# Copies of the attention's key pages, made at other places of a decoder step

## The chip, the cores and the metric

The kernel runs on one core of a Trainium2 chip. The core has five engines that work side by side, each in its own order: TensorE (PE in the profile) multiplies matrices, VectorE (DVE) and ScalarE (ACT) work element by element, GpSimd (POOL) does this more slowly and issues some DMAs, and SyncE (SP) issues most DMAs. The metric is the time of one execution in microseconds, lower is better; a kernel's time is the median of its runs.

## The reference

One inference step of a decoder layer, for a prompt of 1024 tokens and for 8 running sequences with 4 new tokens each (32 "sample" rows, 1056 rows in all). Model width is 1024, everything is in float32. What matters here:

```python
h, gate = modulated_input(x, c, w_ada, b_ada, g_norm)
qa, ka, va, za, qi, ki, wi, qr, kr, vr, zr, ga, gr = split_projection(h @ w_in)
y_a = attn_fn(heads(qa), ka, va, heads(qi), ki, wi) * silu(za)     # sparse attention, 8 heads of 64
ret, ret_state = ret_fn(rotary(qr), rotary(kr) * DK_R ** -0.5, vr) # retention, 8 heads of 64
y_r = group_norm_heads(ret) * g_ret * silu(zr)
merged = sigmoid(ga) * (y_a @ w_pa) + sigmoid(gr) * (y_r @ w_pr)
x = x + gate * (merged @ w_out)
```

The sparse attention scores all keys with a small indexer (4 heads of 64), keeps the best 256 of each query and attends to these. For the sample rows the past keys and values lie in a pool of 80 pages of 128 tokens; a page table of 8 sequences times 8 pages says which page holds what:

```python
ki_past = cache_kidx[page_table].reshape(DB, PAST_LEN, HEAD_DIM_IDX)
kg = where(in_past, cache_k[phys, slot], take_rows(k_new, idx_n))   # phys from page_table
logits = einsum('bqhd,bqkhd->bhqk', q, kg) * HEAD_DIM_A ** -0.5
```

## The kernel before, in words

Each projection is one block of 128 of the weight columns, made for all 1056 rows in three chunks of 352. A product in float32 is made of three products of rounded parts (high times high, low times high, high times low; L226 to L228), so a projection takes 72 matrix products. Its weights are loaded one projection ahead by SyncE (`prefetch`, L205) into two or three buffers and split into their high and low part by ScalarE (L211) and by VectorE or, for every third, GpSimd (L212). `project_parts` runs the chunks and hands each to a function `use(c, p)` that empties the bank.

The stages follow each other in this order, with the times of the profiled execution. The head (0 to 54 us) normalizes and modulates the rows and makes the first projections. The index stage (66 to 140 us) scores the prompt's keys block by block, from row block 7 down to 2, with four heads each (L905 to L915); beside it four gate projections run, and GpSimd gathers the samples' index keys page by page (L951). Retention (145 to about 545 us) runs over four pairs of heads; each has the projections of the attention's queries, of the retention's keys, queries, values and gate, and of two merge gates, 7 projections or 21 chunks, between which its own products stand: score products (L739), products with the state, and at the end of the pair the group norm (L802 to L824), whose rows are turned by TensorE (L821) and multiplied out of the bank by VectorE (L824). Rotation (L691 to L693) is done by GpSimd for the first two pairs and for the keys of the third. In the same stage VectorE and ScalarE count, bit by bit, the threshold of the best 256 scores (`pick_all`; L996 on VectorE, L1003 on ScalarE), one bit behind every two chunks. Then come four key projections and four value projections (560 to 690 us). Between them the samples' past keys are scored: SyncE reads the gathered keys back (L1210), VectorE turns them in blocks of 32 (L1212), TensorE multiplies (L1195), in eight groups of four sequences times a quarter of the past. Gates, the prompt's attention, and the output follow.

The past keys are not read from the pool directly. `copy_page` copies one page of a sequence, 256 KB, from the pool into a scratch array KG in device memory, in the order of blocks in which the keys are read back later. It takes three steps: ScalarE writes one column of the page table into a small tile with two buffers (L582), GpSimd loads the number of the sequence from it into a register (L583), and GpSimd issues the DMA from the page of that number (L584). `project_parts` calls it behind every chunk from the start of retention on, so the 64 copies run behind the first 64 chunks of retention's 84, sequence by sequence. What was left of them would be made ahead of the samples' key stage, by a loop that finds nothing to do.

The order of each engine's instructions is laid out when the kernel is built: a planner takes the instructions in the order of the program text as priorities and places each on its engine as its model of durations lets it be ready. `tc.issue_after(x)` forbids an instruction to be placed ahead of `x` on the same engine; in `copy_page` it keeps ScalarE's write behind the last ScalarE instruction that the program made so far. `marks` keeps the search's steps behind the chunks in the same way.

Of the kernel before, what the change touches and what calls it, by code (L numbers as in the profile page):

```python
# [124 lines left out]
def _hybrid_step(ctx, tc, A, outs, dbg):  # L125
    nc = tc.nc
# [17 lines left out]
    def pj():  # L144

        turns[0] += 1
        if third[0] and turns[0] % 3 == 0:
            return third[0].tile([128, 512], F32, name="pj3", bufs=1)
        return psj.tile([128, 512], F32, name="pj", bufs=2)

    def pl():
        return ps.tile([128, 1024], F32, name="pl", bufs=2)

    def pt():
        return ps.tile([128, 512], F32, name="pt", bufs=2)
# [68 lines left out]
    def terms(p, w, k, sl):  # L224
        wh, wl = w
        nc.tensor.matmul(p, wh[:, k], HH[k][:, sl], start=(k == 0), stop=False)  # L226
        nc.tensor.matmul(p, wh[:, k], HL[k][:, sl], start=False, stop=False)  # L227
        nc.tensor.matmul(p, wl[:, k], HH[k][:, sl], start=False, stop=(k == KT - 1))  # L228
# [16 lines left out]
    def last_on(engine):  # L245
        return next(i for i in reversed(nc.cur_bb.bb.instructions) if i.engine == engine)
# [4 lines left out]
    with ExitStack() as s0:  # L251
# [84 lines left out]
        for k in range(KT):  # L336
            load_wa(k)
            if k in AT:
                i = AT.index(k)
# [33 lines left out]
        rows_, turn = {}, [0]  # L373
# [56 lines left out]
        v, t, u = [RB[:, T + 9 * i:T + 9 * i + 9] for i in range(3)]  # L430
# [62 lines left out]
        for k in range(KT):  # L493
            for step in steps[k].split():
# [3 lines left out]
                else:  # L498
                    at, o = int(step[1]), int(step[2])
# [13 lines left out]
    def prefetch():  # L513

        while order and len(fetched) < (2 if room[0] else 1):
            f0 = order.pop(0)
            room[1] += 1
            pool = room[0] if room[0] and room[1] % 3 == 0 else wp
            with tc.issue_after(loads[-1].ins):
                fetched.append((f0, wload(pool, w_in, f0, 128, bufs=2 if pool is wp else 1)))  # L520
        if fetched:
            f0, ws = fetched.pop(0)
            with tc.issue_after(head_ends[0].ins), tc.issue_after(head_ends[1].ins):
                split.append((f0, wsplit(wp, ws, 128)))
# [7 lines left out]
    def project_parts(f0, use, chunks=chunks):  # L532

        if not split:
            prefetch()
        g0, w = split.pop(0)
        assert g0 == f0
        prefetch()
        for c, sl in enumerate(chunks):
            p = pj()[:, :sl.stop - sl.start]  # L540
            for k in range(KT):
                terms(p, w, k, sl)
            end = last_on(mybir.EngineType.PE)
            use(c, p)
            copy_page()
            if marks is not None:
                marks.append([last_on(e) for e in (mybir.EngineType.DVE, mybir.EngineType.Activation)])
            yield end

    def project(f0, use, chunks=chunks):  # L550
        for _ in project_parts(f0, use, chunks):
            pass
# [20 lines left out]
    KG = dram.tile([NB, 4, 4, 256, 128], F32, name="KG")  # L573
    pages = []

    def copy_page():
        if pages:
            pts, i = pages.pop(0)
            b, g = divmod(i, 8)
            t = cst.tile([NB, 1], I32, name="ptn", bufs=2)  # L580
            with tc.issue_after(last_on(mybir.EngineType.Activation)):
                nc.scalar.copy(t, pts[:, g:g + 1])  # L582
            v = nc.gpsimd.value_load(t[b:b + 1], min_val=0, max_val=A["cache_k"].shape[1] - 1)  # L583
            nc.gpsimd.dma_start(KG[b, g // 2, :, 128 * (g % 2):128 * (g % 2) + 128],  # L584
                              A["cache_k"][0][bass.ds(v, 1)].rearrange("o t (j h) d -> (o j) t (h d)", j=4))


    rows_kept = [2]
# [23 lines left out]
    def retention(gp):  # L612
        with ExitStack() as s3:
            rp = s3.enter_context(tc.tile_pool(name="rp", bufs=1, reuse_waits="tile"))
            RC = rp.tile([128, R_ALL], F32, name="rc")
            nc.sync.dma_start(RC, A["rcs"])
            O = rp.tile([128, 9, 2, 64], F32, name="O")
            nc.gpsimd.memset(O[:, 8], 0.0)
            SD = rp.tile([128, 8, 128], F32, name="SD")
            nc.gpsimd.memset(SD, 0.0)  # L620
            for p in range(4):
                rows = split_rows(gp, O_QA + 128 * p, p, q_rows, qs)
                pair(rp, RC, O, SD, p, rows)
                for _ in rows:
                    pass
                gates(gp, (4 + 2 * p,))
                summed = gate_rows(rp, p)
                gates(gp, (5 + 2 * p,))
                summed()
# [209 lines left out]
    with ExitStack() as s1:  # L839
# [4 lines left out]
        with ExitStack() as s2:  # L844
            ip = s2.enter_context(tc.tile_pool(name="ip", bufs=1, reuse_waits="tile"))
            QS = [ip.tile([128, TT], F32R, name=f"qs{h}") for h in range(4)]
            pts = cst.tile([NB, 8], I32, name="pts")
# [9 lines left out]
            def use_qi(h0):  # L857
                def use(c, p):
                    sl = late[c]
                    for i in (0, 1):  # L860
                        src, q = p[64 * i:64 * i + 64], QS[h0 + i]
                        if c == 1:
                            h = 4 * (h0 + i)
                            for o in (0, 64):
                                nc.vector.tensor_copy(QF[o:o + 64, :, h:h + 4],
                                                      src[:, T - sl.start:].rearrange("p (b i) -> p b i", b=NB))
                        nc.scalar.copy(q[0:64, sl], src)
                        nc.scalar.copy(q[64:128, sl], src)
                        nc.vector.tensor_sub(q[64:128, sl], src, f32(q[64:128, sl]))
                return use  # L870
# [11 lines left out]
            for g in range(3):  # L882
                p = pt().rearrange("p (t c) -> p t c", c=128)
# [10 lines left out]
            nc.vector.tensor_scalar(wsc[:NS, 8], kiw[:NS, 8, 64:68], 0.0625, None, op0=OP.mult)  # L894
            project(O_QI + 128, use_qi(2), late)

            for b in range(7, 1, -1):
                W = (b + 1) * 128
                for h in range(4):
                    m = -(-W // 512)  # L900
                    p = pl().rearrange("p (m c) -> p m c", c=512)[:, :m, :W // m]
                    q = QS[h][:, b * 128:b * 128 + 128]
                    for n in range(m):
                        sl = slice(n * W // m, (n + 1) * W // m)
                        nc.tensor.matmul(p[:, n], q, KH[:, sl], start=True, stop=False)  # L905
                        nc.tensor.matmul(p[:, n], q, KL[:, sl], start=False, stop=True)
                    rl = ip.tile([128, LK], F32, name="rl", bufs=2)
                    nc.scalar.activation(rl[:, :W].rearrange("p (m c) -> p m c", m=m), p, AF.Relu)
                    if h == 0:
                        nc.vector.tensor_scalar(SC[b], rl[:, :W], wsc[:, b, 0:1], None, op0=OP.mult)  # L910
                    else:
                        scored = nc.vector.scalar_tensor_tensor(SC[b], rl[:, :W], wsc[:, b, h:h + 1], SC[b], op0=OP.mult, op1=OP.add)
                if b == 7:
                    whole_row = scored.ins
                nc.vector.tensor_add(SC[b][:, W - 128:W], SC[b][:, W - 128:W], C[:, C_CAUS:C_CAUS + 128])  # L915
# [23 lines left out]
            for G in (0, 1):  # L939
                p = pt()[:, :128]  # L940
                nc.tensor.matmul(p, SX[:NS, 128 * G:128 * G + 128], dw.rearrange("p h t -> p (h t)"), start=True, stop=True)
                t = ip.tile([128, 4, NS], F32, name="wt", bufs=2)
# [4 lines left out]
            for G in (0, 1):  # L947
                KP = []
                for b in range(4 * G, 4 * G + 4):
# [5 lines left out]
                    p = pt()  # L955
# [136 lines left out]
        ps1 = ExitStack()  # L1092
        ps = third[0] = ps1.enter_context(tc.tile_pool(name="psr", bufs=1, reuse_waits="tile", space=PSUM))
        marks = []
        pages.extend((pts, i) for i in range(64))
        retention(gp)
        assert len(marks) == 84
        drain()
# [20 lines left out]
    def token_rows(tl2, x, p, out_p, out_s, dst):  # L1119
        rows = slice(128 * p, 128 * p + 128)  # L1120

        def use(t0, m, n, y):
            tk = tl2.tile([128, 4, 128], F32, name="tk", bufs=2)
            nc.scalar.copy(tk[:n, :m], y[:n, :m])
            if n == 128:
                nc.sync.dma_start(out_p[0, 0, 128 * t0:128 * t0 + 512, 2 * p:2 * p + 2].rearrange("(t p) h d -> p t (h d)", p=128), tk)
            else:
                nc.sync.dma_start(out_s[0, :, :, 2 * p:2 * p + 2].rearrange("b i h d -> (b i) (h d)"), tk[:n, 0])
            if dst is not None:
                nc.sync.dma_start(dst[128 * t0:128 * t0 + m * n, rows].rearrange("(t p) c -> p t c", p=n), tk[:n, :m])  # L1130
        to_tokens(x, use)
# [124 lines left out]
            nc.tensor.matmul(x[:, 16 * p:16 * p + 16], dm[:, 128 * p:128 * p + 128], C[:, C_SB8:C_SB8 + 16], start=True, stop=True)  # L1256
        nc.scalar.copy(YS[:, :, 16 * G:16 * G + 16], x[:, :64].rearrange("p (h c) -> p h c", h=4))

    while pages:
        copy_page()  # L1260
    for p in range(4):
        nc.vector.tensor_tensor(
            QB[:, p].rearrange("p b (h q) -> p b h q", h=8),
# [6 lines left out]
    for p in range(4):  # L1270
        x = tl2.tile([128, TT], F32, name="kx", bufs=1)
        for _ in split_rows(tl, O_KA + 128 * p, p, k_rows, ks, x):
            pass
        token_rows(tl2, x, p, k_out, ks_out, None)
        next(past), next(past)
    for p in range(4):
        x = tl.tile([128, TT], F32, name="raw", bufs=rows_kept[0])
# [274 lines left out]
    for n_, j in enumerate(line):  # L1552
        if j not in merged:
            load_merged(j)
        t, u = merged[j]
# [133 lines left out]
```

## Time and profile before

| | us |
|---|---|
| median of 3 runs (1084.94, 1090.76, 1093.57) | 1090.76 |
| profiled execution | 1085.57 |
| its span, first to last instruction | 1083.9 |
| TensorE busy | 1054.6 (97%) |
| VectorE busy | 694.8 (64%) |
| ScalarE busy | 458.3 (42%) |
| GpSimd busy | 271.4 (25%) |
| mean granted clock of TensorE | 0.989 |
| first and last copy of a page issued | 151.8 and 464.5 |
| a copy, from issue to landing, median | 7.3 |
| first read of the gathered keys issued | 560.3 |

"Busy" is the time in which an engine works on something. An engine's wait is put down to the one instruction that ended last before it could start, "who <- by whom". The granted clock is the share of TensorE's full clock that it was allowed in a stretch. Names like KG or kt are the program's, L584 is a line of the kernel.

### The profile page before, as it was taken

What the parts mean: (1) busy time and instruction counts of PE and PEld (TensorE: products, weight loads), DVE (VectorE), ACT (ScalarE), POOL (GpSimd) and SP (SyncE); (2) the same over time, 40 slices, a digit from 0 to 9 for tenths busy, and PEclk for the clock granted to TensorE, in tenths of its full rate; (3) what the DMA queues carried; (4) which work ended last, traced back from release to release, by engine and by line L of the source; (5) the groups of instructions that cost most, each with busy time, mean ns of one, the idle gap of its engine ahead of it and who ended that gap; (6) DMA issues with size and microseconds to landing.
All of it is one profiled execution on the core that took longest, in us unless ns stands there. A gap on an engine that the chain in (4) does not pass through costs nothing. (4 is left out here: it accounts for less than half of the span.)

```text
span 1083.9 us, 20351 instructions
## 1 busy us (share of the span) xinstructions
PE 1054.6 (97%) x7903; PEld 968.3 (89%) x7903; DVE 694.8 (64%) x1538; ACT 458.3 (42%) x981; POOL 271.4 (25%) x227
## 2 busy tenths in 40 slices
PE   7999999899999999899999999999999999999997
PEld 6899799798989989899999899787999999998776
DVE  6875269677877996699934443311356766597665
ACT  5675354445545455423223322221345665442111
POOL 0013027333834551402110002254023333100000
PEclk9999999799999999999999999999999999999999
DMA  9924256466658674662378779786957520556431
GB/s 308 259 74 130 69 169 166 114 207 176 176 132 236 182 198 127 194 182 80 109 241 298 265 253 309 234 293 240 333 202 267 197 95 31 177 179 241 160 122 59
DMA packets 173620, 202.79 MB, mean 187 GB/s; under 512 B 32068, under 2 KB 140500, under 8 KB 172436
## 3 DMA queue, kind: packets, MB, share of 16 engines
q1 hardware_dynamic: 150352, 164.59, 48.2%
q0 software_dynamic: 22656, 36.05, 10.9%
q8 instruction: 62, 1.02, 0.4%
q10 hardware_dynamic: 516, 0.86, 0.2%
q14 instruction: 34, 0.28, 0.1%
HBM read 156.12 MB, written 57.95 MB: 197 GB/s over the span
## 5 line engine op out<-in xcount | busy, mean ns | idle before, releaser
L226 PE MATMUL pj<-hh,wh 128*128 128x352 f32 (+1 forms) x1168 | 385.3, 330 | 0.0
L228 PE MATMUL pj<-hh,wl 128*128 128x352 f32 (+1 forms) x1168 | 379.8, 325 | 0.2 <-POOL wl L212 0.2
L227 PE MATMUL pj<-hl,wh 128*128 128x352 f32 (+1 forms) x1168 | 379.3, 325 | 0.0
L226 PEld LDWEIGHTS pj<-hh,wh 128*128 128x128 f32 x1168 | 221.1, 189 | 11.6 <-issue 8.0
L228 PEld LDWEIGHTS pj<-hh,wl 128*128 128x128 f32 x1168 | 221.2, 189 | 7.1 <-issue 6.3
L227 PEld LDWEIGHTS pj<-hl,wh 128*128 128x128 f32 x1168 | 221.8, 190 | 3.8 <-issue 3.1
L996 DVE TENSOR_SCALAR_CACHE_REDUCE eq<-sc,cand 128x896 bf16<-128x896 f32 (+4 forms) x155 | 135.7, 875 | 2.6
L211 ACT CAST wh<-ws 128x1024 fp32r<-128x1024 f32 (+1 forms) x65 | 61.1, 941 | 119.6 <-PE pj L227 85.7
L584 POOL DMA_DIRECT2D KG<-in_cache_k x64 | 71.9, 1124 | 127.2 <-issue 55.9
L212 POOL TENSOR_TENSOR wl<-ws,wh 128x1024 fp32r<-128x1024 f32 x18 | 43.3, 2408 | 206.1 <-ACT wh L211 152.1
L212 DVE TENSOR_TENSOR wl<-ws,wh 128x1024 fp32r<-128x1024 f32 (+1 forms) x47 | 54.5, 1160 | 52.3 <-ACT wh L211 52.1
L1374 POOL TENSOR_SCALAR lg<-lg,st 128x1024 f32<-128x1024 f32 (+7 forms) x64 | 47.3, 758 | 110.0 <-DVE st L1371 100.4
L1212 DVE STREAM_TRANSPOSE kt<-kv 128x1024 f32<-128x1024 f32 x32 | 39.0, 1238 | 37.0 <-DMA kv<-KG 36.6
L1366 ACT ACTIVATE lg<-lg,st 128x1024 f32<-128x1024 f32 (+7 forms) x64 | 49.5, 775 | 28.8 <-DVE st L1360 28.8
L1600 PE MATMUL pj<-woh,MH 128*128 128x512 f32 (+1 forms) x136 | 51.4, 378 | 0.0
L1601 PE MATMUL pj<-wol,MH 128*128 128x512 f32 (+1 forms) x136 | 51.2, 377 | 0.0
L1602 PE MATMUL pj<-woh,ML 128*128 128x512 f32 (+1 forms) x136 | 51.2, 377 | 0.0
L1186 POOL DMA_INDIRECT kv<-in_cache_v,idx x32 | 31.8, 992 | 57.8 <-PE sx L1245 40.3
L1003 ACT ACTIVATE ra<-sc,cand 128x1024 bf16<-128x1024 f32 x31 | 35.5, 1146 | 12.9 <-DVE cand L1079 12.9
L1617 ACT ACTIVATE u<-xo 128x512 f32<-128x512 f32 (+2 forms) x19 | 11.6, 609 | 66.0 <-DVE xo L1616 42.7
L831 ACT ACTIVATE raw<-pj 128x352 f32<-128x352 f32 x48 | 22.2, 463 | 38.1 <-PE pj L228 33.7
L1003 ACT ACTIVATE ra<-scs,cand 32x1056 bf16<-32x1056 f32 x31 | 36.4, 1174 | 0.8
(363 smaller groups left out, 1897.7 us busy)
## 6 DMA issues: line engine op xcount, KB each, us to landing
ws<-in_w_in SPq DMA_DIRECT2D x49, 512.0 KB
KG<-in_cache_k POOLq DMA_DIRECT2D x64, 256.0 KB, 7.3
kv<-KG SPq DMA_DIRECT2D x32, 512.0 KB
rot<-in_rot SPq DMA_DIRECT2D x8, 1056.0 KB
x<-in_w_ada SPq DMA_DIRECT2D x16, 512.0 KB
TG<-raw SPq DMA_DIRECT2D x15, 528.0 KB
wst<-in_w_out SPq DMA_DIRECT2D x12, 512.0 KB
u<-TG SPq DMA_DIRECT2D x8, 528.0 KB
```

Source lines behind the costliest of these rows:

```text
L211: nc.scalar.copy(wh[:, :, :n], ws[:, :, :n])
L212: (nc.vector if k == 4 or len(order) % 3 else nc.gpsimd).tensor_sub(wl[:, :, :n], ws[:, :, :n], f32(wh[:, :, :n]))
L226: nc.tensor.matmul(p, wh[:, k], HH[k][:, sl], start=(k == 0), stop=False)
L227: nc.tensor.matmul(p, wh[:, k], HL[k][:, sl], start=False, stop=False)
L228: nc.tensor.matmul(p, wl[:, k], HH[k][:, sl], start=False, stop=(k == KT - 1))
L584: nc.gpsimd.dma_start(KG[b, g // 2, :, 128 * (g % 2):128 * (g % 2) + 128], A["cache_k"][0][bass.ds(v, 1)].rearrange("o t (j h) d -> (o j) ...
L996: nc.vector.tensor_scalar(junk[:n, :W], sc, thr[:n, j:j + 1], 0.0, op0=op, op1=OP.add, accum_out=cnt[:n, j:j + 1])
L1003: nc.scalar.activation(junk[:n, :W], sc, AF.Sign, bias=thr[:n, NV + j:NV + j + 1], scale=-1.0, accum_out=cnt[:n, NV + j:NV + j + 1])
L1366: nc.scalar.activation(l, l, AF.Exp, bias=st[:, i, 1:2], scale=-1.0, accum_out=st[:, i, 3:4])
L1600: nc.tensor.matmul(x, MH[:, k, tk], wh[:, k], start=(k == 0), stop=False)
L1601: nc.tensor.matmul(x, MH[:, k, tk], wl[:, k], start=False, stop=False)
L1602: nc.tensor.matmul(x, ML[:, k, tk], wh[:, k], start=False, stop=(k == KT - 1))
```

## The change

The copies get other places and another order, and their numbers are written one call earlier.

- The list of pages is made in the index stage, ordered as the keys are read back: by group of four sequences, by quarter of the past, by sequence, by page. Before, it was ordered by sequence.
- `copy_page` is called in the index stage behind every second head of row blocks 6 to 2 (10 calls). In projections it is called behind every second chunk: 6 calls in the four gate projections, 42 in retention, 2 in the first key projection. What is left is done in a row behind that projection's token rows.
- A call writes the number of the next page and issues the copy of the page whose number the call before has written. So the first call issues nothing, and 57 copies are issued by the end of retention, 2 in the first key projection, 5 in the row behind it.

```diff
@@ project_parts
             use(c, p)
-            copy_page()
+            turn[0] += 1
+            if turn[0] % 2:
+                copy_page()
@@ copy_page
+    seen, turn = [], [0]
+
     def copy_page():
         if pages:
-            pts, i = pages.pop(0)
-            b, g = divmod(i, 8)
+            at = pages.pop(0)
             t = cst.tile([NB, 1], I32, name="ptn", bufs=2)
             with tc.issue_after(last_on(mybir.EngineType.Activation)):
-                nc.scalar.copy(t, pts[:, g:g + 1])
+                nc.scalar.copy(t, pages_of[0][:, at[1]:at[1] + 1])
+            seen.append((at, t))
+        if len(seen) > (1 if pages else 0):
+            (b, g), t = seen.pop(0)
             v = nc.gpsimd.value_load(t[b:b + 1], min_val=0, max_val=A["cache_k"].shape[1] - 1)
             nc.gpsimd.dma_start(KG[b, g // 2, :, 128 * (g % 2):128 * (g % 2) + 128],
                               A["cache_k"][0][bass.ds(v, 1)].rearrange("o t (j h) d -> (o j) t (h d)", j=4))
+
+    pages_of = []
@@ index stage
+            pages_of.append(pts)
+            pages.extend((b, 2 * u + i) for G in (0, 1) for u in range(4) for b in range(4 * G, 4 * G + 4) for i in (0, 1))
             for b in range(7, 1, -1):
...
                         scored = nc.vector.scalar_tensor_tensor(SC[b], rl[:, :W], wsc[:, b, h:h + 1], SC[b], op0=OP.mult, op1=OP.add)
+                    if h % 2 and b < 7:
+                        copy_page()
@@ ahead of retention
         marks = []
-        pages.extend((pts, i) for i in range(64))
         retention(gp)
@@ ahead of the samples' keys
-    while pages:
-        copy_page()
@@ key projections
         token_rows(tl2, x, p, k_out, ks_out, None)
+        while p == 0 and (pages or seen):
+            copy_page()
         next(past), next(past)
```

## The prediction

> **What bounds the kernel now.** I read the page first, then TensorE's waits, then the stretches of ten microseconds in which those waits lie, and last the timelines around them. The page:
>
> ```profile
> span 1083.9 us, 20351 instructions
> ...
> PE 1054.6 (97%) x7903; PEld 968.3 (89%) x7903; DVE 694.8 (64%) x1538; ACT 458.3 (42%) x981; POOL 271.4 (25%) x227
> ...
> L584 POOL DMA_DIRECT2D KG<-in_cache_k x64 | 71.9, 1124 | 127.2 <-issue 55.9
> ```
>
> TensorE is busy for 97% of the span. The 64 copies that the change moves take 1.12 us each on GpSimd, which is busy for a quarter. So a copy matters only where it makes TensorE late. All of TensorE's waits, longest first:
>
> ```profile
> PE pt L821 <- DVE tmp L824: 6.5, 3, 3.5
> PE px L303 <- DMA x<-in_x_sample: 3.8, 1, 3.8
> PE pb L739 <- DVE tmp L745: 1.9, 2, 1.1
> PE px L303 <- DMA x<-in_x_prompt: 1.9, 1, 1.9
> PE sx L1195 <- DVE kt L1212: 1.6, 1, 1.6
> PE pb L739 <- POOL qrT L693: 1.5, 1, 1.5
> PE pt L661 <- ACT kd L705: 1.4, 1, 1.4
> ...
> PE pt L821 <- POOL O L813: 0.5, 1, 0.5
> ```
>
> The columns are total us, times, longest. The two L303 rows are the start, out of reach of the change. The rest that it can reach is 13.4 us. The granted clock adds to this (columns: length; busy time and count of PE, PEld, DVE, ACT, POOL; granted clock; DMA share; GB/s):
>
> ```profile
> 190.00:200.00 10.00, 7.34 (x91) 6.08 (x93) 9.96 (x21) 5.23 (x11) 7.49 (x8) 0.64 0.64 178
> 200.00:210.00 10.00, 10.00 (x65) 9.55 (x63) 4.46 (x10) 4.89 (x7) 0.56 (x1) 0.67 0.21 61
> ...
> 250.00:260.00 10.00, 10.00 (x52) 9.37 (x51) 9.72 (x24) 4.58 (x10) 2.39 (x3) 0.83 0.74 226
> ...
> 450.00:460.00 10.00, 6.54 (x29) 5.18 (x28) 9.86 (x19) 5.06 (x12) 5.51 (x4) 0.83 0.41 115
> ```
>
> Right behind TensorE's waits the clock falls: 0.64 and 0.67 cost 3.6 and 3.3 us, and each 0.83 costs 1.7 us, 10.3 us together. The Trainium skill ("TensorE: Matmul & The Clock Gate", What's actually happening) says that an idle window of about 3.4 us halves this clock. Here single waits of 1.5 us were enough when two stood close together, so the trace is stricter than the rule.
>
> **Part by part.** Today the copies run one per third of a projection in head pairs 0 to 2. After the change the calls are ten in the index stage, six in the gate projections beside it, 42 in retention (every second third), two in the first key projection, and five in a row behind it. Because a number is written one call before its copy, 57 copies are issued by the end of retention, 2 and then 5 after it. The work per copy is the same: one number, one load of it, one DMA.
>
> *Head pair 0, score products (189 to 206 us).* Here GpSimd is late:
>
> ```profile
> 179.63 2.46 POOL L691 TENSOR_TENSOR qrT<-qrT,rot 128x1056 f32<-128x1056 f32 x1 [4.57 <-ACT ra L1003]
> 182.06 2.47 POOL L692 TENSOR_TENSOR tmp<-tmp,rot 128x1056 f32<-128x1056 f32 x1
> 184.48 1.14 POOL L584 DMA_DIRECT2D KG<-in_cache_k  x1
> 185.64 2.41 POOL L212 TENSOR_TENSOR wl<-ws,wh 128x1024 fp32r<-128x1024 f32 x1
> 188.00 2.42 POOL L693 TENSOR_TENSOR qrT<-qrT,tmp 128x1056 f32<-128x1056 f32 x1
> ```
>
> TensorE's L739 starts at L693's end (the row of 1.5 us). VectorE hangs on the same end:
>
> ```profile
> 184.59 5.87 DVE L1079 TENSOR_SCALAR cand<-base 128x7 int32<-128x7 int32 x1
> ```
> ```profile
> 250.09 0.74 DVE L1079 TENSOR_SCALAR cand<-base 128x7 int32<-128x7 int32 x1
> ...
> 256.98 0.17 DVE L1079 TENSOR_SCALAR cand<-base 128x7 int32<-128x7 int32 x1
> ```
>
> The same seven-element operation takes 0.17 us when GpSimd is silent, 0.74 us beside one copy, and 5.87 us when a copy, a split and a product follow each other; ScalarE's kd (the row of 1.4 us) waits behind it. The stretch loses 1.5 + 1.4 us, 0.8 us of L739's second row (1.9 less 1.1), and 6.9 us of clock: 10.6 us, which is the bound of the gain; the other bound is nothing. At half the rate the copy at 184.48 is there with an even chance: 0.6 us. GpSimd stood idle for 4.57 us before 179.63, which I read as a wait for the rotated rows and the rotary table, whose loads shared the DMA with copies; at the share of 32.0% that copies hold in another such place (below), half of them is 16% of it, 0.7 us. Of the 6.9 us of clock I take one piece of the size of the smaller falls, 1.7 us. Taken: **-3.0 us**.
>
> The Trainium skill ("SBUF — State Buffer", Who interferes with whom) says that GpSimd and a VectorE operation in a two-port mode exclude each other for a whole instruction, so the lock moves with the copies and is not removed; the rows above agree. It adds (SBUF: two separate sides) that VectorE can as well keep GpSimd from writing descriptors. That would stretch single copies and leave the sum as it is.
>
> *The ends of head pairs 0, 1, 2 (247, 351, 451 us).* The three waits of L821 are 6.5 us. The weights of the next projection come late there:
>
> ```profile
> 438.91 1.68 SPq L205 DMA_DIRECT2D ws<-in_w_in  x2
> ```
> ```profile
> 448.68 1.05 ACT L211 CAST wh<-ws 128x1024 fp32r<-128x1024 f32 x1 [8.95 <-DMA ws<-in_w_in]
> ```
> ```profile
> q1 hardware_dynamic: 2028, 1.29, 51.9%
> q0 software_dynamic: 863, 0.96, 32.0%
> ```
>
> The last two rows are the DMA queues from 438.9 to 448.7: packets, MB, share. ScalarE and VectorE work in order, so both stand behind the split of these weights, and L824, which must empty the bank for TensorE, stands behind that. The copies (q0) hold 32.0% of these 9.8 us, 3.1 us. Half the copies bring the weights 1.6 us earlier. That takes 1.6 us each from the two long waits and all of the third (6.5 less 3.5 leaves 3.0 for the two others; I take 2 and 1): 1.6 + 1.6 + 1.0 = 4.2 us; of the two falls of the clock behind them (1.7 us each) I take one. **-5.9 us**, between 0 and -9.9 us (6.5 + 3.4).
>
> *The end of head pair 3 (542 us).* No copy runs there now, and the wait is the row of 0.5 us. With copies at half rate the weights come 1.6 us later: **+1.6 us**, between 0 and 3.5 us (the longest such wait). VectorE is full in that pair, and ten or so copies may each add 0.6 us (0.74 less 0.17) to it; the search that fills it is not what TensorE waits for, so I take nothing, with 1.1 us (the longest wait for L745) as the other end.
>
> *The key projections.* Five copies meet the reads of the gathered keys:
>
> ```profile
> 595.01 1.25 DVE L1212 STREAM_TRANSPOSE kt<-kv 128x1024 f32<-128x1024 f32 x1 [4.32 <-DMA kv<-KG]
> ...
> 596.75 3.70 DVE L1212 STREAM_TRANSPOSE kt<-kv 128x1024 f32<-128x1024 f32 x3
> ```
> ```profile
> 603.12 1.93 PE L1195 MATMUL sx<-kt,QB 128*32 128x256 f32 x32
> ```
>
> In this group the transposes end at 600.45, 2.7 us before TensorE wants them; the last group has nothing to spare (the row of 1.6 us). One copy costs the whole DMA 0.85 us (3.1 us / 0.96 MB x 0.26 MB), five 4.3 us, 1.6 us over the reserve. **+2 us**, between 0 and 4.3 us. On GpSimd they are five times 1.1 us and the load of the number, in a row; a weight split queued behind them is covered by the projection that runs meanwhile; without that cover it would be up to 5 x 1.1 us late. On SyncE nothing is moved.
>
> *The index stage.* Fifteen copies join the eight gathers of index keys. Their queue mates:
>
> ```profile
> POOL kx L951 <- PE pt L957: 13.4, 4, 5.2
> ```
> ```profile
> L582 ACT COPY ptn<-pts x64: 173/185/191, 150.0 to 462.3; 8x1 int32<-8x1 int32 x64
> ```
>
> ScalarE gets fifteen writes of 0.185 us, 2.8 us, GpSimd 15 x 1.12 = 16.8 us, the DMA 15 x 0.85 = 12.8 us. What hides them is that TensorE has gate projections to fill in with: its list has no wait of that stage at all. I take **+1 us**; the ends are nothing and the 13.4 us above, which is the second rival. No gain is possible there.
>
> *The number one call ahead.* It frees GpSimd from waiting for ScalarE, but GpSimd's idle time before copies (127.2 us) is nothing that TensorE's list shows: 0. In exchange ScalarE's next write waits for GpSimd's load of the call just before, not of the one before that, as there are two buffers.
>
> The sum is -3.0 - 5.9 + 1.6 + 2 + 1 = **-4.3 us**. The profiled execution took 1085.57 us (1083.9 of span, 1.7 around it), so its own forecast is 1081.3 us. The median of the three runs is 1090.76 us, 5.2 us above it, and the difference is applied to that: 1086.5, put down as **1086 us**.
>
> **The rivals.** *First, more goes than the sum takes.* If the score products of pair 0 start before the clock falls, and the weights are in time, all 10.6 and all 9.9 us go, and the costs stay 4.6 us: -15.9 us, 1074.9 us. For it: the falls of the clock stand only behind these waits, so a small gain can save a large piece. Against: the copy is 1.1 of 8 us in GpSimd's chain, and a table load, a split and two weight loads at once remain.
>
> *Second, slower: ScalarE is held by GpSimd in the index stage.* GpSimd waits there for TensorE to free the gathers' two buffers (13.4 us in four waits). A copy's load queued behind such a wait holds the number's buffer; ScalarE's next write waits for it; the rectified scores stand behind that write, and TensorE's score banks, two of them, fill up. If all four waits pass on, they cost 13.4 us and four falls of the clock of the smaller size (6.8 us): 20.2 us, with the forecast's -4.3 us 1106.7 us. It makes the kernel slower by more than 1% from 15.2 us on, three quarters of it. For it: the buffer has one call less to spare. Against: the order of the queues is laid out at build with these loads known, and the longest of the four is 5.2 us, of which TensorE's other work in the stage can hide a part.
>
> *Third, the transfers are late for another reason.* Two weight loads, stored rows and the copies share the queues; if the 0.5 MB loads are as late without half the copies, both gains are nothing and the costs of the keys and the index stage (3 us) stay: 1093.8 us. For it: q1 alone holds 51.9%. Against: q0's 32.0% is too much to be free.
>
> **How the numbers follow.** Chances: forecast 0.43, first rival 0.24, second 0.13, third 0.20. One per cent is about what a measurement of this kernel can tell from no change; the three runs spread from 1084.94 to 1093.57. Faster by over 1% (under 1079.9 us) is the first rival and 0.05 of the forecast's tail: 0.29. Slower by over 1% is the second and 0.03, for the order of all queues is laid out anew: 0.16. Within: 0.55. The range goes from 1071 us, the first rival with 4 us of the runs' spread, to 1103 us, where the second rival is partly in: it leaves out about 0.07 below and 0.12 above. The forecast with the third rival alone would go from 1079 to 1097.
>
> **What would show it.** Right: L821's waits under 3 us in all, L693 of pair 0 ending earlier and no 0.64 behind it, a wait at 542 us of about 2 us, L1195's waits between 2 and 5 us. Wrong: waits of TensorE between 66 and 140 us for ScalarE (second rival), weights that still take 9 us to land (third), or a copy that waits for reads of the keys already issued.

## The result and the profile after

The changed kernel takes 1077.83 us, the median of 4 runs (1076.89 to 1078.88), where the kernel before took 1090.74 us beside it: a ratio of 0.989, with a 95% interval from 0.985 to 0.993. Measured once more later, on 6 runs beside 18 of the kernel before, it took 1080.43 us (1077.99 to 1083.03), a ratio of 0.993 [0.991, 0.995]. So it is faster by 0.7 to 1.1%, some 9 to 13 us. The forecast was 1086 us in a range from 1071 to 1103; for the profiled execution it was 1081.3 us, and that took 1076.89 us. The ratios below leave out three executions that ran slower than the others of their kernel (1164.38 us of the kernel before, 2081.31 us with the number ahead alone, 1092.67 us at full rate), while the medians count them.

The page of the changed kernel (busy time, share, instructions; for a group of instructions busy us, mean ns, idle time before it):

```profile
span 1075.2 us, 20361 instructions
...
PE 1049.0 (98%) x7903; PEld 962.2 (89%) x7903; DVE 697.6 (65%) x1538; ACT 458.9 (43%) x981; POOL 271.3 (25%) x227
...
L590 POOL DMA_DIRECT2D KG<-in_cache_k x64 | 72.7, 1136 | 229.3 <-issue 102.4
```

The span is 8.7 us shorter. TensorE's instructions are the same 7903, and they are busy 5.6 us less. The clock is the likely reason: by the stretches below it loses 6.9 us less. GpSimd does the same work. The line numbers have moved: the copy is L590 (was L584), the rotation L699 to L701 (L691 to L693), the score products L747 and their VectorE step L753 (L739, L745), the turning at a pair's end L829 with L832 (L821, L824), the transposes L1223 (L1212).

TensorE's waits (total us, times, longest us):

```profile
PE pb L747 <- DVE tmp L753: 4.5, 3, 1.9
...
PE pt L669 <- ACT kx L607: 2.0, 2, 1.0
PE sx L1206 <- DVE kt L1223: 1.5, 1, 1.5
PE pt L829 <- POOL O L821: 0.9, 1, 0.9
PE pt L969 <- DMA kx<-in_cache_kidx,gidx: 0.7, 1, 0.7
PE pt L735 <- ACT kd L713: 0.7, 1, 0.7
...
PE pt L829 <- DVE tmp L832: 0.2, 1, 0.2
```

The list's first row of before, 6.5 us at the ends of the pairs, is now its last one here, 0.2 us. The products' wait for VectorE has grown from 1.9 to 4.5 us instead: 1.6 us in pair 0, 1.0 us in pair 2 and 1.9 us in pair 3, where the kernel before had none. The key projections' wait for ScalarE (L669, 2.0 us) has this row before:

```profile
PE pt L661 <- ACT kx L599: 1.2, 2, 0.9
```

The same stretches as before and one that is new (length; busy time and count of PE, PEld, DVE, ACT, POOL; granted clock; DMA share; GB/s):

```profile
190.00:200.00 10.00, 7.72 (x111) 6.67 (x104) 9.20 (x22) 4.67 (x9) 3.11 (x3) 0.89 0.54 154
200.00:210.00 10.00, 10.00 (x86) 9.22 (x84) 5.73 (x18) 5.82 (x10) 1.13 (x1) 0.94 0.11 31
250.00:260.00 10.00, 10.00 (x65) 10.00 (x64) 7.73 (x19) 4.46 (x9) 1.11 (x1) 1.00 0.49 138
450.00:460.00 10.00, 10.00 (x65) 10.00 (x64) 9.83 (x31) 2.47 (x6) 1.12 (x1) 1.00 0.84 251
490.00:500.00 10.00, 8.09 (x117) 7.16 (x116) 9.93 (x13) 3.18 (x7) 2.65 (x3) 0.91 0.29 86
500.00:510.00 10.00, 10.00 (x84) 9.59 (x83) 9.83 (x16) 3.19 (x5) 0.00 (x0) 0.92 0.06 15
```

Between 190 and 210 us the clock was 0.64 and 0.67; it is 0.89 and 0.94, so the loss went from 6.9 to 1.7 us. At 250 and 450 us it was 0.83 and is full: 3.4 us more. New is a fall between 490 and 510 us, 0.9 + 0.8 = 1.7 us, behind a wait of 1.9 us of the score products of pair 3. GpSimd's timeline in pair 0 (start, length, instruction, what ended its idle time):

```profile
178.36 2.46 POOL L699 TENSOR_TENSOR qrT<-qrT,rot 128x1056 f32<-128x1056 f32 x1 [4.45 <-DMA tmp<-qrT]
180.79 2.46 POOL L700 TENSOR_TENSOR tmp<-tmp,rot 128x1056 f32<-128x1056 f32 x1
183.32 2.46 POOL L701 TENSOR_TENSOR qrT<-qrT,tmp 128x1056 f32<-128x1056 f32 x1
185.74 2.41 POOL L212 TENSOR_TENSOR wl<-ws,wh 128x1024 fp32r<-128x1024 f32 x1
188.09 1.13 POOL L590 DMA_DIRECT2D KG<-in_cache_k  x1
```

The rotated queries are ready at 185.78 us, where it was 190.42, which is 4.6 us earlier. Only 1.27 us of this is an earlier start of the first step. The rest is the chain itself, 7.4 us long instead of 10.8: no copy (1.14 us) lies between the steps, and the weight split (2.41 us) now follows the last one. In a second profile of the changed kernel (the last run below) the chain is as short again, but it starts no earlier than in the kernel before:

```profile
179.93 2.46 POOL L699 TENSOR_TENSOR qrT<-qrT,rot 128x1056 f32<-128x1056 f32 x1 [4.81 <-DVE eq L1008]
...
184.88 2.46 POOL L701 TENSOR_TENSOR qrT<-qrT,tmp 128x1056 f32<-128x1056 f32 x1
187.30 2.69 POOL L212 TENSOR_TENSOR wl<-ws,wh 128x1024 fp32r<-128x1024 f32 x1
```

The weights at the end of pair 2, SyncE's first issue and the split that waits for them:

```profile
429.67 0.38 SPq L205 DMA_DIRECT2D ws<-in_w_in  x1
```
```profile
435.80 1.05 ACT L211 CAST wh<-ws 128x1024 fp32r<-128x1024 f32 x1 [5.31 <-DMA ws<-in_w_in]
```

The split starts 6.1 us behind the issue instead of 9.8. In that stretch the copies' queue holds 17.6% of the DMA, where it was 32.0%.

### The profile page after: what moved, and what is told of

The parts are those of the page before. It is cut to its first block, busy times and chain, and to the rows that moved or that the text cites. A ratio compares the mean times of both kernels' runs of the same rounds, so it can differ in the third digit from the quotient of the medians.

```text
span 1075.2 us, 20361 instructions
## 1 busy us (share of the span) xinstructions
PE 1049.0 (98%) x7903; PEld 962.2 (89%) x7903; DVE 697.6 (65%) x1538; ACT 458.9 (43%) x981; POOL 271.3 (25%) x227
## 5 line engine op out<-in xcount | busy, mean ns | idle before, releaser
L590 POOL DMA_DIRECT2D KG<-in_cache_k x64 | 72.7, 1136 | 229.3 <-issue 102.4
L1223 DVE STREAM_TRANSPOSE kt<-kv 128x1024 f32<-128x1024 f32 x32 | 39.2, 1239 | 34.7 <-DMA kv<-KG 34.3
```

## The experiments

Each ratio is against runs of the kernel before on the same chip and at the same time, whose medians lay between 1089.09 and 1091.04 us.

**No copies.** The keys are read from fixed pages of the pool, in the same amounts, so they aren't those of the page table.

```diff
     def copy_page():
-        if pages:
...
+        pass
...
-                    nc.sync.dma_start(kk, KG[4 * G + b4, u].rearrange("j (t s) c -> (j t) s c", s=8))
+                    f0 = 2 * (4 * (4 * G + b4) + u)
+                    nc.sync.dma_start(kk, A["cache_k"][0][f0:f0 + 2].rearrange("g t h d -> (g t h d)").rearrange("(j t s c) -> (j t) s c", j=4, t=32, s=8))
```

> The kernel before without any copies: no number, no load, no DMA, and the samples' past keys are read, in the same pieces, from fixed pages of the pool, so that part of the sample attention is computed on wrong keys. Theory: this is the floor of the change; the weights at the pair ends land in 4 to 6 us, no wait of L821 over 0.5 us, 1068 to 1076 us, that is 2 to 10 us under the changed kernel. Rival B: no lower than the changed kernel, 1076 us or more, with waits elsewhere.

It took 1065.34 us, 0.978 [0.976, 0.979], 2.7 us under the lowest time expected: 24.6 us is all that the copies, with their numbers and their place in the queues, cost the kernel before. TensorE's waits:

```profile
PE sx L1186 <- DVE kt L1204: 1.6, 1, 1.6
...
PE pt L812 <- POOL O L804: 0.3, 1, 0.3
```

No wait at the ends of pairs 0 to 2 is left, and none for GpSimd's rotation. The split of the weights at pair 2's end:

```profile
427.78 1.05 ACT L211 CAST wh<-ws 128x1024 fp32r<-128x1024 f32 x1 [3.81 <-DMA ws<-in_w_in]
```

Their load was issued at 423.15 us, so they are there after 4.6 us. The change brings 9 to 13 of the 24.6 us.

**GpSimd's time without the traffic.** The kernel before, with the number written and loaded as it was, but in place of the DMA GpSimd clears a tile twice, 1.1 us in all. The keys come from fixed pages.

```diff
-            nc.gpsimd.dma_start(KG[b, g // 2, :, 128 * (g % 2):128 * (g % 2) + 128],
-                              A["cache_k"][0][bass.ds(v, 1)].rearrange("o t (j h) d -> (o j) t (h d)", j=4))
+            for _ in (0, 1):
+                with tc.issue_after(last_on(mybir.EngineType.Pool)):
+                    nc.gpsimd.memset(BI[7].bitcast(F32), 0.0)
...
```

> The kernel before, number and load as they are, but in the place of each copy's DMA GpSimd clears a tile twice (about 1 us together), and the past keys are read from fixed pages, so that part of the sample attention is computed on wrong keys. It keeps GpSimd's time of the copies and takes their traffic away. Theory, as the sum had it: most of the loss is the traffic (5.9 of 8.9 us), so the waits of L821 nearly vanish and the time is within 5 us of the kernel without copies; the score products of pair 0 stay late (2 to 4 us of waits near 190). Rival C (GpSimd's time is the loss): 1086 to 1092 us.

It took 1064.71 us, 0.977 [0.972, 0.982], as little as without copies. GpSimd's timeline in pair 0:

```profile
172.68 2.47 POOL L691 TENSOR_TENSOR qrT<-qrT,rot 128x1056 f32<-128x1056 f32 x1 [2.90 <-DVE base L1077]
175.10 2.49 POOL L692 TENSOR_TENSOR tmp<-tmp,rot 128x1056 f32<-128x1056 f32 x1
177.52 0.54 POOL L585 MEMSET bi<- 128x512 f32 x1
178.00 2.46 POOL L693 TENSOR_TENSOR qrT<-qrT,tmp 128x1056 f32<-128x1056 f32 x1
180.40 0.54 POOL L585 MEMSET bi<- 128x512 f32 x1
180.88 2.48 POOL L212 TENSOR_TENSOR wl<-ws,wh 128x1024 fp32r<-128x1024 f32 x1
```

A clear stands between the steps as a copy did, and it costs nothing: the chain starts at 172.68 instead of 179.63 us, and it ends 10 us earlier, since the weight split now follows it here as well. The waits of 2 to 4 us near 190 us that were expected did not come. What made the chain start late was what it waits for, the rotated rows and the rotary table, whose loads shared the DMA with the copies. The other profiles agree: in all five kernels that issue no copy between 145 and 172 us it starts between 172.44 and 173.73 us, and in the others, at half and at full rate, between 177.27 and 183.42. VectorE is still held by GpSimd, though less than before; its seven-element operation over the whole search, in the kernel before, here, and without copies (busy us, mean ns):

```profile
L1079 DVE TENSOR_SCALAR cand<-base 128x7 int32<-128x7 int32 x30 | 20.4, 681 | 0.9
```
```profile
L1079 DVE TENSOR_SCALAR cand<-base 128x7 int32<-128x7 int32 x30 | 13.5, 450 | 0.9
```
```profile
L1070 DVE TENSOR_SCALAR cand<-base 128x7 int32<-128x7 int32 x30 | 9.5, 315 | 0.8
```

Of the 10.9 us that the copies add to it, the clears leave 4.0, and those cost no time that was measured. That the other 6.9 us cost nothing either was not tried apart from the traffic.

**The traffic without GpSimd.** ScalarE issues each copy in its own queue, from a fixed page; GpSimd and the number have no part in it.

```diff
...
             with tc.issue_after(last_on(mybir.EngineType.Activation)):
-                nc.scalar.copy(t, pts[:, g:g + 1])
-            v = nc.gpsimd.value_load(t[b:b + 1], min_val=0, max_val=A["cache_k"].shape[1] - 1)
-            nc.gpsimd.dma_start(KG[b, g // 2, :, 128 * (g % 2):128 * (g % 2) + 128],
-                              A["cache_k"][0][bass.ds(v, 1)].rearrange("o t (j h) d -> (o j) t (h d)", j=4))
+                nc.scalar.dma_start(KG[b, g // 2, :, 128 * (g % 2):128 * (g % 2) + 128],
+                                  A["cache_k"][0][i:i + 1].rearrange("o t (j h) d -> (o j) t (h d)", j=4))
```

> The kernel before, but ScalarE issues each copy itself, from a fixed page, at the same places; no number, no load, nothing on GpSimd, so that the copied keys are those of wrong pages. It keeps the traffic and takes GpSimd's part away. Theory: weights still land late at the pair ends (8 to 10 us), the waits of L821 stay at 4 to 8 us, the waits near 190 shrink: 1083 to 1089 us. Rival C: 1070 to 1078 us, as without copies.

It took 1108.25 us, 1.018 [1.013, 1.023], slower than the kernel before, and both expectations missed. The copies' line (ns least, median, most) and TensorE's waits:

```profile
L581 ACTq DMA_DIRECT2D KG<-in_cache_k x64: 598/2494/5860, 144.7 to 480.9; - x64
```
```profile
PE pt L658 <- ACT tmp L674: 9.8, 4, 4.0
PE pt L658 <- ACT vtok L699: 6.1, 2, 3.2
```

Issuing one copy occupies ScalarE for 2.5 us in the median, up to 5.9, and TensorE waits for ScalarE. So it adds a cost of its own and tells nothing of the traffic alone; the run above does that.

**The number one call ahead, alone,** in the kernel before; and **the changed kernel without it.**

```diff
@@ in the kernel before
...
+            seen.append((b, g, t))
+        if len(seen) > (1 if pages else 0):
+            b, g, t = seen.pop(0)
...
@@ in the changed kernel
-        if len(seen) > (1 if pages else 0):
+        if seen:
```

> The kernel before, its copies at their old places and in their old order, only with each number written one call ahead. Theory: 1090 us within 4, the waits of L821 at the pair ends stay (4 to 8 us in all). Rival A: 1078 to 1083 us. Rival B (any new order of the queues moves the time by this much): anything from 1076 to 1098 us, without a change in how long the weights at the pair ends take to land.

> The changed kernel, but each call writes a page's number and issues the copy of that same page. Theory (fewer copies at a time in retention: weights land earlier, GpSimd's chain is shorter): the number ahead buys nothing, 1078 us within 4, the waits of L821 stay under 1 us in all. Rival A (it is the number ahead that pays, GpSimd no longer stands waiting for ScalarE): most of the gain goes, 1086 to 1092 us, and GpSimd's rotation in pair 0 ends later again.

The first took 1088.49 us, 0.999 [0.997, 1.001]: nothing, though its waits at the pairs' ends are 3.2 us, less than the 4 to 8 expected. The second took 1079.12 us, 0.991 [0.989, 0.994], no other than the changed kernel. The number ahead has no part in the gain.

**The order of the pages, alone,** in the kernel before.

```diff
-        pages.extend((pts, i) for i in range(64))
+        pages.extend((pts, 8 * b + 2 * u + i) for G in (0, 1) for u in range(4) for b in range(4 * G, 4 * G + 4) for i in (0, 1))
```

> The kernel before with nothing changed but the order of its 64 pages (that of the changed kernel). Every instruction has its place and length; only addresses differ. All theories: 1090 us within 3; it shows how far two kernels with the same queues lie apart, and that the order of need by itself is worth nothing while all copies end before the first read.

1089.63 us, 0.999 [0.996, 1.002]: nothing. The places of the copies are what is left.

**The changed kernel at full rate in retention,** sixteen calls ahead of it, 48 behind its first 48 chunks.

```diff
-            if turn[0] % 2:
+            if turn[0] % 2 or marks is not None:
                 copy_page()
```

> The changed kernel, its first sixteen calls in the index stage and the gate projections, then one call behind every chunk of retention until the pages are through (48 chunks: pairs 0 and 1 and a little of pair 2), none in the key projections. Theory: pairs 0 and 1 get their late weights back (landing 8 to 10 us at 245 and 345 instead of 7.3 and 5.9), the end of pair 2 stays free: 1080 to 1087 us. Rival B: no relation between the copies in flight and the landing of the weights.

It took 1083.4 us, 0.995 [0.992, 0.998], with runs from 1075.9 to 1092.67 us; its profile is of the fastest of them, so of its waits only the pattern is used:

```profile
PE pb L747 <- DVE tmp L753: 2.6, 3, 1.4
PE pt L829 <- DVE tmp L832: 1.8, 1, 1.8
```

The wait at the end of pair 0 is back (1.8 us), with the weights 8.7 us under way. Those of pair 1 take 8.7 us too, and nothing waits for them. The wait of pair 3's products is gone; no copy runs there. It gains 6.6 us where the changed kernel gains 9 to 13, so the lower rate may be worth 2 to 6 us, but the intervals overlap.

**The kernel before, its copies begun nine chunks later,** at the same rate of one per chunk.

```diff
-            copy_page()
+            skipped[0] += marks is not None
+            if skipped[0] > 9:
+                copy_page()
...
+    skipped = [0]
```

> The kernel before, with the copies starting behind the tenth chunk of retention in place of the first, at the same rate, so that the first ten microseconds of copies do not stand beside the rotated rows of pair 0. Theory (traffic): the rotation of pair 0 is in time, its 10 us go (waits and half clock near 190), the late weights at the ends of pairs 0 to 2 stay: 1080 to 1085 us. Rival C (GpSimd's own time, not the traffic, makes pair 0 late): it shrinks as well, but so must the waits near 290, where GpSimd rotates for pair 1.

It took 1080.27 us, 0.994 [0.992, 0.996], as little as the second measurement of the whole change. GpSimd in pair 0, then the stretches, then TensorE's waits:

```profile
173.31 2.48 POOL L695 TENSOR_TENSOR qrT<-qrT,rot 128x1056 f32<-128x1056 f32 x1 [6.77 <-DMA tmp<-qrT]
```
```profile
190.00:200.00 10.00, 9.96 (x130) 9.16 (x129) 7.61 (x14) 5.27 (x10) 1.74 (x2) 1.00 0.36 105
...
490.00:500.00 10.00, 4.83 (x92) 4.00 (x90) 9.89 (x10) 2.47 (x5) 4.72 (x4) 0.88 0.44 108
500.00:510.00 10.00, 9.80 (x75) 9.36 (x77) 9.89 (x16) 2.74 (x3) 0.00 (x0) 0.77 0.21 59
```
```profile
PE pb L743 <- DVE tmp L749: 5.1, 3, 3.8
...
PE pt L825 <- DVE tmp L828: 1.9, 3, 1.1
```

With no copy beside the loads of pair 0 the rotation starts at 173.31 us, and the loss there is gone whole. The loss of pair 3 is larger than in the changed kernel: the copies now reach into that pair at full rate. The waits at the pairs' ends fell to 1.9 us although the rate beside them is that of before and the weights take 7.4 to 9.2 us; the theory of the rate said they would stay, so its time came out for a reason that was in part another. The rival looked for waits near 290 us, where the kernel before has none; here they are 2.3 us.

**More copies in the index stage:** 32 calls ahead of retention, in it two behind every five chunks, none behind.

```diff
-            if turn[0] % 2:
+            if marks is None or turn[0] % 5 in (0, 2):
                 copy_page()
...
-                    if h % 2 and b < 7:
+                    if b < 7:
                         copy_page()
```

> The changed kernel with 32 calls ahead of retention (behind every head of row blocks 6 to 2 and behind every chunk of the gate projections) and two calls per five chunks in retention, so that none is left for the key projections. Theory: fewer copies in retention (about 32 instead of 42) and none beside the reads of the gathered keys give 1 to 4 us: 1074 to 1077 us. Against it stands the index stage, whose gathers wait for twice the copies: if the wait of 0.75 us on them grows to 4 us or more, 1078 to 1084 us.

It took 1082.9 us, 0.993 [0.991, 0.995], no gain over the changed kernel. TensorE now waits in the index stage:

```profile
PE pl L976 <- ACT kp L971: 2.7, 1, 2.7
...
PE pt L969 <- DMA kx<-in_cache_kidx,gidx: 2.5, 3, 1.5
```

That is 5.2 us and a fall of the clock behind it. What retention gained (the products' wait for VectorE is 2.6 us instead of 4.5) is given back there.

**The changed kernel, copies in bursts where the DMA is quiet:** in retention none but two behind each of the last two chunks of the gate and four behind each of the first two of the attention's queries; six buffers for numbers. And the same with the index stage's calls behind every head, in blocks 4 to 2 alone.

```diff
-            if turn[0] % 2:
+            if marks is None:
+                calls = turn[0] % 2
+            else:
+                calls = {(O_ZR, 1): 2, (O_ZR, 2): 2, (O_QA, 0): 4, (O_QA, 1): 4}.get((O_ZR if O_ZR <= f0 < O_GA else f0 // 512, c), 0)
+            for _ in range(calls):
                 copy_page()
@@ in the second of the two, besides
-                    if h % 2 and b < 7:
+                    if b < 5:
                         copy_page()
```

> The changed kernel with its sixteen calls ahead of retention, and in retention twelve calls per pair in bursts at the chunks where the kernel without copies leaves the DMA nearly idle (two behind the second and third chunk of the gate projection, four behind the first and second chunk of the attention's queries), none behind rotated rows and merge gates; six buffers for the numbers. Theory (the traffic must not stand beside loads that TensorE waits for): the weights at the pair ends land in 4 to 6 us, the waits near 190, 390 and 495 shrink: 1068 to 1074 us, 4 to 10 us under the changed kernel. Rival (bursts hurt as much as a steady rate, since GpSimd and ScalarE are held for 7 us at a time): 1076 to 1086 us.

> As the one before, but in the index stage the calls stand behind every head of row blocks 4 to 2, when most gathers are done, not behind every second head of row blocks 6 to 2; all copies end in retention. Theory: the wait of 0.75 us on the gathers goes, and the key projections have no copy: 1 to 2 us under the one before, 1066 to 1073 us. Rival: the index stage's later part has its own waits, 1072 to 1080 us.

They took 1083.82 us, 0.996 [0.994, 0.998], and 1079.89 us, 0.993 [0.990, 0.995]. TensorE's waits in the first, and three stretches of the second:

```profile
PE pj L219 <- DMA ws<-in_w_ada: 6.1, 3, 2.6
PE pj L219 <- ACT raw L843: 3.9, 2, 2.5
```
```profile
225.00:235.00 10.00, 6.88 (x57) 6.29 (x58) 7.11 (x24) 4.52 (x9) 3.21 (x2) 0.83 0.92 289
328.00:338.00 10.00, 6.77 (x58) 5.62 (x56) 4.88 (x23) 5.94 (x11) 0.83 (x1) 0.83 0.86 271
433.00:443.00 10.00, 6.86 (x58) 6.22 (x58) 4.67 (x19) 4.64 (x9) 2.14 (x1) 0.83 0.94 312
```

L219 multiplies blocks of `w_ada` for the layer's own gate, between the two merge gates of a pair. The changed kernel does not wait for them in retention; here they are late, and so is ScalarE in emptying the bank of the merge gate before (L843). That is about 10 us in each of the two kernels, and in the second the clock falls to 0.83 at the ends of pairs 0 to 2. Both theories missed, by 10 and by 7 us. Both times lie in their rivals' ranges, but no wait of the index stage, which the second rival named, is in that kernel's list. The quiet places stand just ahead of these loads, and the DMA is busy for 0.86 to 0.94 of the stretches shown; that the bursts made the loads late is read from this and was not tried apart.

**The changed kernel again,** beside the last four.

> The changed kernel once more, as the measure for the two bursts: 1078 us within 2.

1080.43 us, as given above, 0.4 us over what was expected. Its profile has the same waits: 6.0 us for VectorE at the products, since that of pair 0 is 3.1 us instead of 1.6, and 0.5 us for it at the pairs' ends.

## Why the prediction was right, and where it was not

It was right in direction and in most of the places where time would go. The time lies in its range, at the bound between faster and the same by 1%. The forecast was 4.4 us too high for the profiled execution, and 6 to 8 us for the medians. By its steps, each from the waits and the clock of the two profiles:

| step | forecast | before to after |
|---|---|---|
| pair 0, score products | -3.0 | -6.5 |
| ends of pairs 0 to 2 | -5.9 | -9.7 |
| end of pair 3 | +1.6 | +0.4 |
| products of pair 3 | 0 | +3.6 |
| key projections | +2 | +0.7 |
| index stage | +1 | +0.7 |

The table's last column sums to -10.8 us, the span fell by 8.7; the other 2.1 us lie in smaller gaps, 0.2 us of them in pair 2's products, and are not placed further. The two gains together came out at 16.2 us instead of the 8.9 of the sum, the costs at 5.4 instead of 4.6. Of the signs that the prediction named, the wait near 542 us (0.9 us instead of about 2) and the one for the turned keys (1.5 us instead of 2 to 5) did not come.

*Pair 0.* The waits there (1.47, 1.40 and 0.79 us) became 0.66 and 1.62, and the clock's loss of 6.8 us (0.66 over the 20 us from 190) became 1.7 us. The step that failed in size is "of the 6.9 us of clock I take one piece": all but one piece went. In kind, "GpSimd is late" was right, but its reasons were weighed wrongly. The copy within the chain was priced at 0.6 us, and the weight split beside it was taken to remain ("1.1 of 8 us" leaves it out: by the prediction's own rows the chain is 10.8 us long). Without both the chain is 3.4 us shorter, in both profiles of the changed kernel. That is what the change brought here. It is read from the traces; why the planner laid the split behind the chain was not tried. The shared DMA was priced at 0.7 us, and the chain did start 1.27 us earlier in one profile and 0.30 us later in the other. This reason is worth much more than its price, only not to this change: with GpSimd kept as busy and the traffic gone the chain started 6.95 us earlier, and with the first nine chunks free of copies 6.3 us earlier (173.31 for 179.63). Half the rate does not reach that.

*The ends of the pairs.* "Half the copies bring the weights 1.6 us earlier": they came 1.6, 4.1 and 3.6 us earlier (8.91, 10.00 and 9.77 became 7.31, 5.90 and 6.13), which is more than the copies' share of the queues (3.1 us, halved) gives. The share is no price for the delay: without any copies the weights took 4.6 us at the end of pair 2, 5.1 less than before, though the copies held the DMA for 3.1. How much of the -9.7 us is due to the rate is less sure than the two profiles say: the kernels with the number ahead or the order alone, timed as no change, wait 3.2 and 3.7 us there, not 6.5. Measured from these the gain in waits is about 3 us; three profiles with the changed places (0.2, 0.5 and 0.3 us) agree. That the waits shrank in the kernel that begins later, at the old rate, shows that something else counts as well: the copies' phase against the loads, or the order of the queues that was laid out anew. Which, is open.

*Pair 3.* The end was priced at +1.6 and cost 0.4 us. The cost came in the products instead, which the prediction had at nothing, with 1.1 us as the other end: 1.9 us of wait with 1.7 of clock. VectorE is busy 9.8 to 10.0 of every 10 us there, and was before. "The search that fills it is not what TensorE waits for" failed: in VectorE's queue the step after the product stands behind the search. That the copies bring the wait is not shown. It grows with the copies issued between 460 and 500 us in some profiles (none gave no such wait at full rate, 2 gave 0.3 us, 4 gave 1.2, 5 gave 1.9, 7 gave 1.6 and 3.8). But of the three kernels that issue one copy there, all with the old places, two have no such wait, and the third, with the number ahead alone, has this:

```profile
PE pb L744 <- DVE tmp L750: 1.4, 1, 1.4
```

There the order of the queues is new too, so such an order may bring most of the wait by itself.

*Key projections and index stage.* The five copies beside the reads of the keys were priced at 1.6 us over the reserve. That did not come: L1206 waits 1.5 us, not more than before, and the 0.7 us came at ScalarE's copies of the keys. In the index stage the one wait is 0.7 us, for a gather, near what was taken. The other end of that step is real all the same: 32 calls instead of 16 ahead of retention cost 5.2 us and a fall of the clock.

*The number ahead* was put at 0, and both runs on it say 0.

*The rivals.* The first, that more goes, describes pair 0 and the pairs' ends best: 16.2 of its 20.5 us went, its clock argument being the reason. What stayed of them, 4.3 us, and the cost in pair 3 kept the time from its 1074.9 us. The second did not come: no wait for ScalarE in the index stage. The third, that the transfers are late for another reason, falls with the run without copies, where they are early.

*The clock.* The Trainium skill ("TensorE: Matmul & The Clock Gate", What's actually happening) has an idle window of about 3.4 us for a halved clock. The profile after is again stricter than the rule: 1.9 us of idle in pair 3 were enough for a loss of 1.7 us. Not every such wait was followed by a fall: the wait of 1.4 us just shown was not.

## What to carry to other kernels

A background transfer is priced by what is loaded beside it and is wanted soon, not by the time that its issue takes on an engine: here 64 pairs of clears, 67 us on GpSimd in place of 72 us of issuing, cost nothing that could be measured, and the copies 25 us. Before spreading such transfers, find the few loads whose lateness reaches TensorE, and keep these stretches free; half the rate everywhere did no more than leaving out the first nine chunks, and in bursts at quiet places TensorE waited for the next loads. Look also at what stands between the steps of a late chain: in pair 0 the changed kernel's traces show a weight split of 2.4 us laid behind it. Where a stall is followed by a lower clock, count the clock's loss as part of what there is to gain, for in pair 0 5.1 of the 6.5 us were clock. And profile more than one kernel that is timed as no change: the same waits came out at 6.5, 3.7 and 3.2 us.

## What the runs showed of the hardware that was not expected

- The issue of one 256 KB copy between two places of device memory held ScalarE's instruction stream for 0.6 to 5.9 us, 2.5 in the median. The same copy from GpSimd took 1.11 to 1.19 us in the kernel before.
- A fall of the clock can be worth more than the waits beside it: in pair 0 of the kernel before, with 3.7 us of waits, the clock was 0.50 from 192.86 to 206.51 us, a loss of 6.8 us; in the changed kernel, with 2.3 us of waits, it was 0.50 from 197.84 to 201.25 us, a loss of 1.7. A wait of 2.46 us at 439 us in the first kernel with bursts was followed by none (1.00 from 433 to 443).
- A pair of 0.5 MB loads took 4.6 us without copies, 6.1 us where the copies held 17.6% of the DMA's time and 9.8 us where they held 32.0%.
- The recorded clock of a whole execution need not follow its time: with the order alone the profile gives 0.940 on average at 1088.24 us, the kernel before 0.989 at 1085.57.
